# Two layers of a hybrid-attention transformer: remainders on GpSimd, queries split in whole tiles, and another order of the head groups' units

## The chip, the core and the metric

The kernel runs on one core of a Trainium2 chip. The metric is the device time of one execution in microseconds (us). The core has five engines, each with a queue that is worked off in order: TensorE (PE; its weight loads are shown as PEld), VectorE (DVE), ScalarE (ACT), GpSimd (POOL) and SyncE (SP), which here issues all transfers.

## The reference

Two layers of one trunk over 512 latent tokens (x) and 256 context tokens (ctx), width 1024, everything in float32. A layer is: modulation from SiLU(c) and SiLU(c_ctx); an RMS norm; one input projection of 3072 columns, split among four groups of heads; a mixer for each group; one output projection over the four results with a gated residual; an RMS norm and a squared-ReLU MLP of width 4096. Cut to what matters here:

```python
hx = rms_norm(x, p['norm1_g']) * (1 + sc1x) + sh1x
hc = rms_norm(ctx, p['norm1_g']) * (1 + sc1c) + sh1c
(lw_q, lw_k, lw_v, lf_q, lf_k, lf_v, lr_q, lr_k, lr_v, lr_g, ln_q, ln_k, ln_v) = split_in(hx @ p['w_in'])
...
out_w = window_attention(q, k, v, k_c, v_c, p['a_sink'])          # A
out_f = rms_norm(diff_attention(q, k, v, k_c, v_c, lam), ...)     # B
out_r = rms_norm(o_f + flip(o_b), p['c_gn_g']) * gate             # C
out_n = neighbourhood_attention(q, k, v, k_c, v_c, p['d_rpb'])    # D
mix_x = jnp.concatenate([...], axis=-1) @ p['w_out']
x = x + g1x * mix_x
x = x + g2x * squared_relu_mlp(h2, p['w_mlp1'], p['w_mlp2'])
```

A is windowed attention with a sink, B differential attention (two softmaxes of 32-wide halves, one subtracted from the other), C retention in both directions (no softmax, a decay table), D attention over a neighbourhood. In the second layer the context tokens only serve as keys and values.

## The kernel before

**Two parts for one number.** A matrix product in full precision is made of three in the format fp32r: every operand is split into a part hi (ScalarE copies the tile into fp32r) and a remainder lo = operand - hi (`split`, lines 275 and 276; the remainder by VectorE). `gemm` (lines 315 to 317) adds hi x hi, hi x lo and lo x hi. Activations h are held as pairs hh, hl; a weight tile (128 output columns by 1024 inputs) comes in two loads of 128x512, each into a buffer wr, and is split into wh and wl (`wload`). There are five buffers wr, which the loads of the modulation's weights share, and four each of wh and wl. In a layer's attention stage 24 weight tiles of the input projection and the first six eighths of eight tiles of the output projection pass through `wload`.

**Units.** Each group's work is cut into units: a0, b0, b1, c0, c1, d0, d1 (A has one, the others two of two heads each). A unit has an input part (`in_a` to `in_d`: its tiles of the input projection, norms, rotary tables, splits) and an attention part (`at_a` to `at_d`). `weave` runs the attention parts in the order `ORDER`, here a0 b0 b1 c0 c1 d0 d1, and lets the input parts of the following units, then the output projection (`out_ac`), run ahead of them by given leads. From the program written in this order, a scheduler sets the order of the instructions on each engine at build time; the engines then wait for each other by semaphores.

**Stacks.** A score is a product over 64 numbers (32 for B), so hi and lo of a query stand one above the other on the 128 partitions (`qs`), and the keys' hi (`ks`) and lo (`kl`) twice each. For A, C and D, `qstack` lets ScalarE write hi of a head's half tile and VectorE the remainder straight onto the other half (line 600); `kstack` does the same on one half (lines 608 and 610) and has the other half copied by a transfer from SBUF to SBUF (`KCOPY`, line 634, issued by SP), four for a tile. For B, `stack32` splits the whole tile into two tiles sp and puts four stacks together by 16 transfers of 32 partitions.

**Norms of heads.** `rstd` makes mean squares on TensorE (lines 241 and 243), `finish` the inverse roots on ScalarE and VectorE, which two products a piece (line 257) spread over the partitions again. Queries and keys of A, B and D pass through this on the way in, the outputs of B and C at the end of their unit (`headnorm`).

**GpSimd** does four small memsets and nothing else. In the MLPs, the weights go through the same `wload`.

## Time and profile before

| | |
|---|---|
| time, median of 3 runs | 1898.29 us (1894.59 to 1900.06) |
| the profiled execution | 1897.64 us, span of its instructions 1895.6 us |
| mean granted clock of TensorE | 0.990 |
| start and first norm | 0 to 70 us |
| attention stage, layer 0 | 70 to 540 us |
| MLP, layer 0 | 540 to 1090 us |
| attention stage, layer 1 | 1090 to 1560 us |
| MLP, layer 1 | 1560 to 1895.6 us |

The page of the profile gives each engine's busy time. [...] The timeline has each instruction with its start and length; in square brackets stands how long its engine was idle before it and what ended that. TensorE's instructions overlap, so the distance between two starts is what one takes of the engine's time, and the length shown is longer.

### The profile page before, as it was taken

The page shows a single profiled execution, that of the slowest core. Times are in us where ns is not written, and L with a number is a line of the kernel's source. Part 1 is how long each engine was busy: PE and PEld are TensorE (multiplying, and loading weights), DVE is VectorE, ACT ScalarE, POOL GpSimd, SP SyncE. Part 2 cuts the span into 40 slices and gives each one's busy share as a digit, 9 for nine tenths or more (in the row PEclk, how much of TensorE's full clock was granted, in tenths as well). Part 3 has the DMA queues.
Part 4 walks back from the last instruction along what each step waited for, and adds up shares of the span by engine and source line. Part 5 has one row for each costly group of instructions (what it writes and reads, how often), then busy time and mean ns, then how long its engine had stood idle before and what let it go on. Part 6 is the DMA issues. An engine that isn't in the chain of part 4 may idle for free.

```text
span 1895.6 us, 29665 instructions
## 1 busy us (share of the span) xinstructions
PE 1843.1 (97%) x10899; PEld 1519.8 (80%) x10899; DVE 1307.4 (69%) x3005; ACT 973.4 (51%) x1934; POOL 0.2 (0%) x4
## 2 busy tenths in 40 slices
PE   7998889999999999999999999999899999999999
PEld 3786667778878888888888777878677788989897
DVE  5788867788777847847847367898788764545453
ACT  4677656668654214223323356877577763334242
POOL 0000000000000000000000000000000000000000
PEclk8999989999999999999999999999899999999999
DMA  8324334432323523423422352332243223232322
GB/s 297 99 79 122 100 120 131 148 95 65 109 95 106 157 93 117 151 95 117 150 95 89 111 172 83 83 96 79 85 133 95 75 95 100 90 100 90 100 90 95
DMA packets 110417, 208.68 MB, mean 110 GB/s; under 512 B 14272, under 2 KB 20160, under 8 KB 110272
## 3 DMA queue, kind: packets, MB, share of 16 engines
q1 hardware_dynamic: 110272, 206.78, 34.7%
q8 instruction: 86, 1.41, 0.3%
q14 instruction: 59, 0.48, 0.1%
HBM read 182.09 MB, written 5.24 MB: 99 GB/s over the span
## 4 chain that ended last, share of the span: by engine, by line
PE 89%; ACT 5%; DVE 3%; DMA 2%; issue 1%; SPq 0%; ACTq 0%; DVEq 0%
PE mm L315 23%; PE mm L317 23%; PE mm L316 23%; PE ps L697 3%; PE po L703 2%; PE po L705 2%; PE ps L262 1%; PE ps L850 1%; PE pt L241 1%; ACT pth L275 1%; PE pt L257 1%; PE pt L869 1%; PE pt L798 1%; ACT P L856 1%; DMA zm<-in_dd_dram 1%
## 5 line engine op out<-in xcount | busy, mean ns | idle before, releaser
L275 ACT ACTIVATE wh<-wr 128x512 fp32r<-128x512 f32 (+1 forms) x414 | 252.9, 614 | 645.3 <-PE mm L316 605.0
L317 PE MATMUL mm<-hh,wl 128*128 128x512 f32 (+2 forms) x1680 | 548.8, 327 | 6.7 <-DVE wl L276 6.6
L315 PE MATMUL mm<-hh,wh 128*128 128x512 f32 (+2 forms) x1680 | 551.2, 328 | 3.0 <-ACT zq L651 1.7
L316 PE MATMUL mm<-hl,wh 128*128 128x512 f32 (+2 forms) x1680 | 549.8, 327 | 0.0
L276 DVE TENSOR_TENSOR wl<-wr,wh 128x512 fp32r<-128x512 f32 (+1 forms) x414 | 275.4, 667 | 162.4 <-ACT wh L275 156.4
L315 PEld LDWEIGHTS mm<-hh,wh 128*128 128x128 f32 x1680 | 318.3, 190 | 39.9 <-issue 7.6
L317 PEld LDWEIGHTS mm<-hh,wl 128*128 128x128 f32 x1680 | 318.9, 190 | 34.7 <-DVE wl L276 7.7
L316 PEld LDWEIGHTS mm<-hl,wh 128*128 128x128 f32 x1680 | 318.0, 189 | 28.1 <-issue 3.5
L316 PE MATMUL mm<-ml,wh 128*128 128x512 f32 (+1 forms) x768 | 273.2, 356 | 0.0
L315 PE MATMUL mm<-mh,wh 128*128 128x512 f32 (+1 forms) x768 | 272.7, 356 | 0.0
L317 PE MATMUL mm<-mh,wl 128*128 128x512 f32 (+1 forms) x768 | 272.4, 355 | 0.0
L316 PEld LDWEIGHTS mm<-ml,wh 128*128 128x128 f32 x768 | 145.2, 189 | 24.5 <-issue 4.5
L315 PEld LDWEIGHTS mm<-mh,wh 128*128 128x128 f32 x768 | 145.2, 189 | 21.9 <-issue 0.4
L317 PEld LDWEIGHTS mm<-mh,wl 128*128 128x128 f32 x768 | 145.1, 189 | 21.2 <-issue 1.2
L394 DVE SCALAR_TENSOR_TENSOR acc<-wm,silp,acc 128x512 f32<-128x512 f32 x196 | 138.9, 747 | 21.9 <-DMA wm<-in_wmod_dram 21.7
L1127 DVE SCALAR_TENSOR_TENSOR x<-mm,modc,x 128x512 f32<-128x512 f32 (+1 forms) x96 | 63.4, 660 | 116.6 <-PE mm L317 116.6
L703 PE MATMUL po<-pth,vv 128*128 128x256 f32 (+2 forms) x328 | 105.5, 328 | 8.9 <-ACT pth L275 8.1
L276 DVE TENSOR_TENSOR ptl<-pt,pth 128x512 fp32r<-128x512 f32 (+3 forms) x148 | 92.4, 630 | 27.9 <-ACT pth L275 26.4
L275 ACT ACTIVATE pth<-pt 128x512 fp32r<-128x512 f32 (+3 forms) x148 | 80.2, 547 | 32.2 <-PE pt L869 21.6
L1111 DVE TENSOR_TENSOR zq<-mm,nacc 128x256 f32<-128x256 f32 (+1 forms) x128 | 61.9, 484 | 44.5 <-PE mm L317 43.0
L703 PEld LDWEIGHTS po<-pth,vv 128*128 128x128 f32 x328 | 61.8, 189 | 32.3 <-ACT pth L275 24.0
L705 PE MATMUL po<-ptl,vv 128*64 128x256 f32 (+2 forms) x256 | 78.3, 318 | 2.9 <-DVE ptl L276 2.3
(251 smaller groups left out, 2701.3 us busy)
## 6 DMA issues: line engine op xcount, KB each, us to landing
wr<-in_w_dram SPq DMA_DIRECT2D x272, 256.0 KB, 2.6
wm<-in_wmod_dram SPq DMA_DIRECT2D x112, 256.0 KB, 2.8
wr<-in_win_dram SPq DMA_DIRECT2D x96, 256.0 KB, 3.0
wr<-in_wmodh_dram SPq DMA_DIRECT2D x48, 256.0 KB, 3.3
...
zm<-in_dd_dram SPq DMA_DIRECT2D x16, 256.0 KB, 3.5
```

The source lines that it names most:

```text
L241: T.matmul(pj, lhsT=gmean[w], rhs=sq[:, 256 * j:256 * j + 256], start=True, stop=add is None)
L275: S.activation(hi, src, AF.Copy)
L276: V.tensor_tensor(lo, src, hi.bitcast(F32), op=OP.subtract)
L315: T.matmul(p, lhsT=wh, rhs=ah[:, s:s + l], start=(k == 0), stop=False)
L316: T.matmul(p, lhsT=wh, rhs=al[:, s:s + l], start=False, stop=False)
L317: T.matmul(p, lhsT=wl, rhs=ah[:, s:s + l], start=False, stop=(k == len(act) - 1))
L394: V.scalar_tensor_tensor(acc[:, v], r, sil[:, k, v:v + 1], acc[:, v], op0=OP.mult, op1=OP.add)
L697: T.matmul(o, lhsT=x, rhs=y, start=(i == 0), stop=(i == 1))
L703: T.matmul(po[:, c0:c0 + l], lhsT=vv[:, hh, t], rhs=ph, start=start, stop=stop)
L705: T.matmul(po[0:64, c0:c0 + l], lhsT=vv[:, hh, t, 0:64], rhs=pl, start=False, stop=False)
L1111: V.tensor_tensor(r[:, s:s + l], p[:, :l], y2[:, s:s + l], op=OP.mult)
L1127: V.scalar_tensor_tensor(xx, p, modc[:, 40 + m, s // 512:s // 512 + 1], xx, op0=OP.mult, op1=OP.add)
```

## The change

- `split` takes the engine of the remainder as an argument. GpSimd (PL) makes the remainders of the weights in the attention stages (`wrest`; in the MLPs VectorE as before), of all queries and keys, and of the six outputs that `out_ac` splits; it also adds C's two tables (`ctables`). The remainders of the probabilities, of the values and of the norms stay on VectorE.
- Queries and keys of all groups are split as whole tiles into two tiles sp (`parts_of`) and put together by transfers (`stack`): a query tile of A, C or D takes four transfers of 64 partitions, a key tile eight. B's stay 16 of 32 partitions.
- There are six buffers zq instead of five (sp, squares, rotated tiles).
- `ORDER` is a0 c0 b0 c1 b1 d0 d1 in both layers. The numbers that `weave` takes for leads and costs are the same.

```diff
@@ -80,7 +80,7 @@
 PTB = 2
 PSB = 2
 POB = 1
-ZQ = 5
+ZQ = 6
 U3 = 20
 MID = 14
 WPRI = 40
@@ -100,7 +100,7 @@
 CD1 = 11
 TAILC = 10000.0
 MP = 7
-ORDER = ['a0 b0 b1 c0 c1 d0 d1', 'a0 b0 b1 c0 c1 d0 d1']
+ORDER = ['a0 c0 b0 c1 b1 d0 d1', 'a0 c0 b0 c1 b1 d0 d1']
 
 
 def weave(units, ins, ats, cost_in, cost_at, tail, lead, boost):
@@ -154,7 +154,7 @@
 @with_exitstack
 def body(ctx: ExitStack, tc, A):
     nc = tc.nc
-    V, S, G, T, SY = nc.vector, nc.scalar, nc.gpsimd, nc.tensor, nc.sync
+    V, S, PL, T, SY = nc.vector, nc.scalar, nc.gpsimd, nc.tensor, nc.sync
 
     cons = ctx.enter_context(tc.tile_pool(name="cons", bufs=1))
     main = ctx.enter_context(tc.tile_pool(name="main", bufs=1))
@@ -271,9 +271,11 @@
             V.scalar_tensor_tensor(sq[:, s:s + l], ap, EPS if eps else 0.0, sq[:, s:s + l], op0=OP.add, op1=OP.mult)
         V.scalar_tensor_tensor(sq[:, :n], sq[:, :n], -3.0, e3[:, :n], op0=OP.add, op1=OP.mult)
 
-    def split(src, hi, lo):
+    def split(src, hi, lo, eng=V):
         S.activation(hi, src, AF.Copy)
-        V.tensor_tensor(lo, src, hi.bitcast(F32), op=OP.subtract)
+        eng.tensor_tensor(lo, src, hi.bitcast(F32), op=OP.subtract)
+
+    wrest = [PL]
 
     def wload(src, k0=0, k1=8, dst=None):
 
@@ -288,7 +290,7 @@
                 hi = wp.tile([128, 512], F32R, name=nm("wh"), tag="wh", bufs=WB)
                 lo = wp.tile([128, 512], F32R, name=nm("wl"), tag="wl", bufs=WB)
             with tc.high_priority(offset=WPRI):
-                split(r, hi[:, :128 * n], lo[:, :128 * n])
+                split(r, hi[:, :128 * n], lo[:, :128 * n], wrest[0])
             res += [(hi[:, 128 * k:128 * k + 128], lo[:, 128 * k:128 * k + 128]) for k in range(n)]
         return res
 
@@ -467,6 +469,7 @@
         rb = rowb[:, L, :]
         modc = modcs[L]
 
+        wrest[0] = PL
 
         att = ExitStack()
         ap_ = att.enter_context(tc.tile_pool(name=f"att{L}", bufs=1))
@@ -591,44 +594,40 @@
 
         HALF = (slice(0, 64), slice(64, 128))
 
+        def parts_of(t, n):
+
+            hl = [main.tile([128, 768], F32R, name=nm("sp"), tag="zq", bufs=ZQ)[:, :n] for _ in range(2)]
+            split(t[:, :n], *hl, PL)
+            return hl
+
+        def stack(hl, n, r, order):
+
+            x, w = u3r("st"), r.stop - r.start
+            for i, o in enumerate(order):
+                KCOPY(x[w * i:w * i + w, :n], hl[o][r])
+            return x
+
         def qstack(t, n):
 
-            st = (u3r("qs"), u3r("qs"))
-            for h, x in enumerate(st):
-                a, b = HALF[h], HALF[1 - h]
-                S.activation(x[a, :n], t[a, :n], AF.Copy)
-                V.tensor_tensor(x[b, :n], t[a, :n], x[a, :n].bitcast(F32), op=OP.subtract)
-            return st
+            hl = parts_of(t, n)
+            return [stack(hl, n, r, (0, 1)) for r in HALF]
 
         def kstack(t, n):
 
-            st, lo = (u3r("ks"), u3r("ks")), (u3r("kl"), u3r("kl"))
-            for h, (x, y) in enumerate(zip(st, lo)):
-                a, b = HALF[h], HALF[1 - h]
-                S.activation(x[a, :n], t[a, :n], AF.Copy)
-                KCOPY(x[b, :n], x[a, :n])
-                V.tensor_tensor(y[a, :n], t[a, :n], x[a, :n].bitcast(F32), op=OP.subtract)
-                KCOPY(y[b, :n], y[a, :n])
-            return st, lo
+            hl = parts_of(t, n)
+            return [[stack(hl, n, r, (i, i)) for r in HALF] for i in range(2)]
 
         def quarter(i):
             return slice(32 * i, 32 * i + 32)
 
-        def stack32(t, n, order):
-
-            parts = [main.tile([128, 768], F32R, name=nm("sp"), tag="zq", bufs=ZQ)[:, :n] for _ in range(2)]
-            split(t[:, :n], *parts)
-            st = [u3r("st") for _ in range(4)]
-            for i, x in enumerate(st):
-                for r, w in enumerate(order):
-                    KCOPY(x[quarter(r), :n], parts[w][quarter(i)])
-            return st
-
         def qstack32(t, n):
-            return stack32(t, n, (0, 1, 0, 1))
+
+            hl = parts_of(t, n)
+            return [stack(hl, n, quarter(i), (0, 1, 0, 1)) for i in range(4)]
 
         def kstack32(t, n):
-            return stack32(t, n, (0, 0, 1, 1))
+            hl = parts_of(t, n)
+            return [stack(hl, n, quarter(i), (0, 0, 1, 1)) for i in range(4)]
 
         def KCOPY(dst, src):
             SY.dma_start(out=dst.bitcast(F32), in_=src.bitcast(F32))
@@ -912,7 +911,7 @@
                 SY.dma_start(out=tw[:, 0:512], in_=A['dd'][:, 1920 + 512 * t:2432 + 512 * t])
                 S.activation(tw[:, 0:512], tw[:, 0:512], AF.Exp, scale=nlb)
                 S.activation(tx[:, t], tx[:, t], AF.Exp, scale=lf)
-                V.tensor_tensor(tx[:, t], tx[:, t], tw[:, 0:512], op=OP.add)
+                PL.tensor_tensor(tx[:, t], tx[:, t], tw[:, 0:512], op=OP.add)
             return tb, tx
 
         def in_c(u):
@@ -1035,7 +1034,7 @@
             osp = []
             for c in range(6):
                 hi, lo = htile("oh"), htile("ol")
-                split(of[c][:, :nq], hi[:, :nq], lo[:, :nq])
+                split(of[c][:, :nq], hi[:, :nq], lo[:, :nq], PL)
                 osp.append((hi, lo))
             for m in range(8):
                 xr = u3("xr")
@@ -1055,6 +1054,7 @@
         cost_at = {x: c * 1e3 for x, c in zip('abcd', [[CA0, CB0, CC0, CD0], [CA1, CB1, CC1, CD1]][L])}
         weave(units, ins, ats, cost_in, cost_at, out_ac(), [[L0_0, L0_1, L0_2, L0_3, L0_4, L0_5, L0_6, L0_7], [L1_0, L1_1, L1_2, L1_3, L1_4, L1_5, L1_6, L1_7]][L], lambda: tc.high_priority(offset=BOOST))
         att.close()
+        wrest[0] = V
 
 
         mlp = ExitStack()
```

**On SP.** In these rows, wr is a weight load (L284 before, L286 after: projections; L373 and L375: modulation), and st<-sp, ks<-ks and kl<-kl are the transfers of the stacks. Before, where the queries of b1 (sp_2502, sp_2503) and the keys of c0 are put together:

```order
L634 DMA st_2509<-sp_2502 32x768
L634 DMA st_2509<-sp_2503 32x768
L634 DMA ks_2711<-ks_2711 64x768
L634 DMA kl_2713<-kl_2713 64x768
L634 DMA ks_2712<-ks_2712 64x768
L634 DMA kl_2714<-kl_2714 64x768
L284 DMA wr_2751<-in_win_dram 128x512
```

After, the end of the 16 transfers of b0's queries (sp_2399, sp_2400):

```order
L633 DMA st_2418<-sp_2399 32x768
L633 DMA st_2418<-sp_2400 32x768
L286 DMA wr_2445<-in_win_dram 128x512
L286 DMA wr_2451<-in_win_dram 128x512
L375 DMA wr_2559<-in_wmodh_dram 128x512
```

The next weights stand behind the transfers in both; after, the weights of the tile mm_2457 (c1's keys) are the first ones behind b0's queries, and both halves of that tile stand there.

**On TensorE, the end of b0 in layer 0.** The products of the output's norm (L241, L243; spread by L257). Before:

```order
L703 MATMUL po_2810<-pth_2816,vv_1291 128x256
L241 MATMUL ps_2839<-zm_2836,gmean_75 32x256
L243 MATMUL ps_2839<-ident,lsq_2833 32x128 x2
L241 MATMUL ps_2839<-zm_2836,gmean_75 32x256
L243 MATMUL ps_2839<-ident,lsq_2833 32x128 x2
L241 MATMUL ps_2839<-zm_2836,gmean_75 32x256
L243 MATMUL ps_2839<-ident,lsq_2833 32x128 x2
L257 MATMUL ps_2838<-rr_2840,spread 128x256
```

After (L684 transposes values, L344 is the modulation, L317 to L319 is `gemm`):

```order
L243 MATMUL ps_3473<-ident,lsq_3467 32x128 x2
L684 MATMUL pt_3722<-ident,zq_3718 128x128 x4
L344 MATMUL mm_3745<-wr_3737,silp 32x256
L684 MATMUL pt_3732<-ident,zq_3718 128x128 x2
L344 MATMUL mm_3745<-wr_3737,silp 32x256
L344 MATMUL mm_3745<-wr_3739,silp 32x256 x2
L344 MATMUL mm_3745<-wr_3741,silp 32x256
L257 MATMUL ps_3472<-rr_3474,spread 128x256
```

Before, nothing stands between the mean squares and the spread; after, six transposes and five small products do, and tile mm_3771 follows.

**On TensorE, the end of c0 in layer 0, after.** Scores are L696, probabilities times values L701 to L704:

```order
L702 MATMUL po_2328<-pth_2603,vv_1164 128x512
L704 MATMUL po_2328<-ptl_2604,vv_1164 64x512
L701 MATMUL po_2328<-ptl_2627,vv_1164 64x512
L702 MATMUL po_2328<-pth_2626,vv_1164 128x512
L702 MATMUL po_2641<-pth_2647,vv_1164 128x256
L704 MATMUL po_2641<-ptl_2648,vv_1164 64x256
L701 MATMUL po_2641<-ptl_2671,vv_1164 64x256
L702 MATMUL po_2641<-pth_2670,vv_1164 128x256
L317 MATMUL mm_2457<-hh_217,wh_2447 128x512
L318 MATMUL mm_2457<-hl_218,wh_2447 128x512
```

The last products of c0 come right before tile mm_2457, whose weights are those behind the 16 transfers above.

**The weights' remainders in layer 1.** On VectorE before, at the end of b0's attention (L600 a query remainder, L933 and L934 c0's gate):

```order
L600 TENSOR_TENSOR qs_14141<-zq_14138,qs_14141 64x512
L879 TENSOR_TENSOR of_13829<-po_14011,ev_14087 64x256
L853 TENSOR_SCALAR sm_14111<-sm_14111 128x2
L853 TENSOR_SCALAR sm_14090<-sm_14090 128x2
L933 SCALAR_TENSOR_TENSOR zq_14184<-zq_14184,zq_14187 128x512
L903 TENSOR_SCALAR zm_14198<-gp_14194,lg_11949 128x128
L934 SCALAR_TENSOR_TENSOR gt_14183<-gt_14183,gsc_11929,zq_14184 128x512
L904 TENSOR_SCALAR gp_14194<-gp_14194,nlg_11983 128x128
L276 TENSOR_TENSOR wl_14427<-wr_14424,wh_14426 128x512
```

On GpSimd after, in layer 1:

```order
L276 TENSOR_TENSOR wl_13910<-wr_13907,wh_13909 128x512
L276 TENSOR_TENSOR sp_13683<-zq_13679,sp_13682 128x768
L276 TENSOR_TENSOR wl_14024<-wr_14021,wh_14023 128x512
L276 TENSOR_TENSOR sp_14012<-zq_14009,sp_14011 128x512
L276 TENSOR_TENSOR wl_14030<-wr_14027,wh_14029 128x512
```

There the weights' remainders (wl) share a queue with those of queries and keys (sp) alone: 128 wl, 30 sp, 12 of the outputs and 16 sums of tables in both layers.

## Rows read from the trace of the kernel before

**Rows 1.** Page, busy time of each engine, share of span, instructions.
```profile
PE 1843.1 (97%) x10899; PEld 1519.8 (80%) x10899; DVE 1307.4 (69%) x3005; ACT 973.4 (51%) x1934; POOL 0.2 (0%) x4
```

**Rows 2.** Stretches: us, busy PE, PEld, DVE, ACT, POOL, clock, DMA share, GB/s.
```profile
70.00:234.00 164.00, 154.52 (x1014) 124.27 (x1012) 134.98 (x416) 119.90 (x271) 0.00 (x0) 1.00 0.36 101
234.00:256.00 22.00, 14.04 (x53) 9.13 (x54) 11.79 (x32) 9.00 (x20) 0.00 (x0) 0.69 0.36 107
256.00:540.00 284.00, 279.51 (x1718) 224.27 (x1716) 226.44 (x546) 190.94 (x406) 0.00 (x0) 1.00 0.36 112
1090.00:1330.00 240.00, 236.09 (x1390) 189.41 (x1388) 192.57 (x507) 165.79 (x340) 0.00 (x0) 1.00 0.35 102
1330.00:1358.00 28.00, 20.27 (x88) 15.28 (x87) 23.72 (x60) 15.86 (x33) 0.00 (x0) 0.82 0.32 95
1358.00:1560.00 202.00, 199.38 (x1128) 156.06 (x1127) 154.53 (x348) 142.89 (x293) 0.00 (x0) 1.00 0.32 99
```

**Rows 3.** Timeline, layer 0, 234 to 256 us: start, length, idle time before.
```profile
239.58 0.58 SPq L284 DMA_DIRECT2D wr<-in_win_dram  x1
...
240.78 1.06 PE L241 MATMUL ps<-zm,gmean 128*32 128x256 f32 x2 [1.79 <-ACT zm L817]
...
247.15 0.61 ACT L275 ACTIVATE wh<-wr 128x512 fp32r<-128x512 f32 x1
...
247.29 1.28 PE L257 MATMUL ps<-rr,spread 96*128 96x256 f32 x6 [2.87 <-ACT rr L275]
```

**Rows 4.** Timeline, layer 1, 1331 to 1352 us, VectorE and TensorE.
```profile
1331.62 0.69 DVE L600 TENSOR_TENSOR qs<-zq,qs 64x512 fp32r<-64x512 f32 x1
...
1334.47 0.67 DVE L276 TENSOR_TENSOR wl<-wr,wh 128x512 fp32r<-128x512 f32 x1
...
1335.19 0.79 PE L317 MATMUL mm<-hh,wl 128*128 128x512 f32 x1 [3.17 <-DVE wl L276]
...
1349.34 0.95 DVE L610 TENSOR_TENSOR kl<-zq,ks 64x768 fp32r<-64x768 f32 x1
...
1350.41 0.67 DVE L276 TENSOR_TENSOR wl<-wr,wh 128x512 fp32r<-128x512 f32 x1
...
1351.14 0.80 PE L317 MATMUL mm<-hh,wl 128*128 128x512 f32 x1 [3.39 <-DVE wl L276]
```

**Rows 5.** Groups by form on VectorE, 70 to 540 us: busy us, mean ns.
```profile
L276 DVE TENSOR_TENSOR wl<-wr,wh 128x512 fp32r<-128x512 f32 x48 | 32.7, 684 | 6.3 <-ACT wh L275 6.2
...
L276 DVE TENSOR_TENSOR ptl<-P,pth 128x512 fp32r<-128x512 f32 x24 | 16.4, 685 | 2.9 <-ACT pth L275 2.8
...
L600 DVE TENSOR_TENSOR qs<-zq,qs 64x768 fp32r<-64x768 f32 x12 | 11.4, 953 | 1.6 <-ACT qs L599 1.2
...
L610 DVE TENSOR_TENSOR kl<-zq,ks 64x768 fp32r<-64x768 f32 x10 | 9.5, 950 | 0.6 <-ACT ks L608 0.4
...
L667 DVE TENSOR_TENSOR zq<-zq,pt 128x512 f32<-128x512 f32 x11 | 7.6, 687 | 6.1 <-PE pt L257 6.1
```

**Rows 6.** Groups by form on ScalarE, 70 to 540 us.
```profile
L275 ACT ACTIVATE sp<-zq 128x768 fp32r<-128x768 f32 x4 | 3.3, 837 | 2.8 <-DVE zq L667 2.8
```

**Rows 7.** Timeline of SP's transfers between SBUF tiles, layer 0.
```profile
73.61 1.16 SPq L634 DMA_DIRECT2D kl<-kl  x2
...
103.89 11.28 SPq L634 DMA_DIRECT2D st<-sp  x16
...
176.41 10.05 SPq L634 DMA_DIRECT2D st<-sp  x16
```

**Rows 8.** DMA issues: count, KB each, median us to landing.
```profile
wr<-in_win_dram SPq DMA_DIRECT2D x96, 256.0 KB, 3.0
...
ks<-ks SPq DMA_DIRECT2D x20, 192.0 KB, 2.9
```

**Rows 9.** Timeline of TensorE in layer 0's MLP: start and length.
```profile
702.30 0.39 PE L317 MATMUL mm<-hh,wl 128*128 128x512 f32 x1
702.53 0.39 PE L315 MATMUL mm<-hh,wh 128*128 128x512 f32 x1
```

## Prediction

> **What bounds the kernel now.** TensorE is busy for 97% of the span and VectorE for 69% [rows 1], so the most that a change can win is what TensorE loses. The table by stretches says where that is: I leave out the start (0 to 70 us) and the two MLPs, since the change leaves them as they are but for four weight remainders, and look at the two attention stages, which are 940 us of the span. TensorE is busy there for 903.8 us of 940, idle for 36.2 us [rows 2]. The idle time is not spread evenly: 8.0 us of it lie in 22 us of layer 0 (234 to 256 us) and 7.7 us in 28 us of layer 1 (1330 to 1358 us), and only these two stretches have a mean granted clock under 1.00, of 0.69 and 0.82 [rows 2]. [...] In time at full speed that is up to 0.31 x 22 = 6.8 us and 0.18 x 28 = 5.0 us; only the share in which TensorE was busy counts (0.64 and 0.72), so 4.4 and 3.6 us. The two places cost about 12.4 and 11.3 us, the rest of both stages has 20.5 us of idle time.
>
> The timeline says why. In layer 1 TensorE waits twice, 3.17 and 3.39 us, for a weight remainder wl. VectorE made each in 0.67 us, but took it up only behind a query remainder (L600, 0.69 us) and other work the first time, and directly behind a key remainder (L610, 0.95 us) the second time [rows 4]: an engine that works in order had the weights in the wrong place of its queue. In layer 0 unit b0 ends: its norm's chain makes TensorE wait 1.79 us and 2.87 us, and there is nothing to fill it, since the next weights were issued by SP only at 239.58 us, behind 20 copies, and ScalarE reached them at 247.15 us [rows 3].
>
> **The change part by part.** *Remainders leave VectorE.* In the attention stages these go: 128 weight remainders (112 of 512 columns, 16 of 256), 112 x 0.684 + 16 x 0.34 = 82 us; 24 query remainders, 12 x 0.953 and 12 shorter ones at about two thirds, 19 us; 20 key remainders x 0.95 = 19 us; B's eight splits, 16 table sums and twelve output splits, about 28 us by the same times per column [rows 5]. VectorE's 744 us of 940 (79%) [rows 2] become about 596 (63%). Directly on the path lie the two waits of layer 1: 6.6 us of idle time and 3.6 us of clock. GpSimd's queue holds 186 remainders and nothing else, so the weights no longer stand behind scores and gates. Something else on VectorE is late next there (the next ptl), so I take 9 of the 10.2 us (bounds 5 and 10).
>
> What one remainder takes on GpSimd no row shows. Below I bound it with VectorE's own time, 0.68 us for 512 columns and 0.95 us for 768, and with twice that; I take 1.7 us for 768 columns, near the upper end, because for the sum only a late remainder matters. All 186 are 131 us at the lower bound and 261 us at the upper, 14 to 28% of 940 us: GpSimd does not become the bound. [...]
>
> The relief acts on the other 20.5 us of idle time as well, where TensorE waits for short steps of VectorE and ScalarE. I take 12 us of it (bounds 0 and 18), since VectorE's free time rises from 21 to 37%.
>
> *B alternates with C.* b0 is now followed by c1 and not by b1. At b0's end the products of tile mm_3771 stand next, with weights that SP issued before any copy, and six transposes and five products lie inside the norm's chain; so 12.4 us go and some 3 us of the 4.7 us of waits [rows 3] stay: -9.4 us.
>
> The same kind of hole opens elsewhere. In the new SP order all 16 copies of b0's queries stand ahead of wr_2445, the next weights (before, one tile of weights was fetched ahead of such a block). From the last spread product on, the chain is: VectorE's two products, 0.69 + 0.41 us [rows 5]; ScalarE's copy 0.84 us [rows 6]; GpSimd's remainder 1.7 us, of which one copy's issue hides 0.6; 16 copies 10.6 us (10.05 to 11.28) [rows 7]; landing 3.0 us [rows 8]; wh 0.6 us [rows 3]. Sum 17.2 us. TensorE has between these the tail of c0: 12 products of 512 columns at 0.23 us [rows 9], eight of 256 at half of it, and six narrow ones, together 4.3 us. So it loses 12.9 us, and with the same clock loss as in the hole before (4.4 us) 17 us. Bounds: 11.6 (remainder at 0.95 us, 10.05 us of copies, full clock) and 18.2.
>
> Elsewhere in c0 and c1 of layer 0 some seven chunks stand without input products between them. One chunk costs VectorE two operations of 0.685 us [rows 5], TensorE 4 x 0.23 = 0.92 us; 7 x 0.45 = 3 us (bounds 0 and 6).
>
> *Queries in whole tiles.* Each of 12 query tiles of A, C and D now goes over four copies, where ScalarE and VectorE wrote the stacks directly, and each of 10 key tiles over eight instead of four: 88 more, at 0.58 us of SP each [rows 7] 51 us, plus a landing of 2.9 us [rows 8]. In most places another unit's attention covers this. It is open where the unit follows at once: a0 in both layers, and d1, four tiles; about 1.3 us each, +5 us (bounds 0 and 12). A wait of SP here holds up the weight loads that stand behind it. ScalarE wins a little, since one copy of 0.84 us [rows 6] takes the place of two as long: nothing on the path.
>
> The sum: -9 - 12 - 9.4 + 17 + 3 + 5 = -5.4 us. The profiled execution took 1897.64 us (span 1895.6), 0.65 us under the median of 1898.29 us, so 1897.64 - 5.4 = **1892 us**.
>
> **The rivals.** *More of the idle time goes.* If the relief is at its bound (18 us), the queries' copies are all covered and the hole is at its lower bound, it gives 1892 - 6 - 5 - 5 = about 1876 to 1880 us. For it: VectorE is the engine that both other waits in layer 1 end at [rows 4]. Against: the order has more stretches without input products in layer 0 than before.
>
> *The relief is given back at a shared port.* VectorE keeps some 190 operations with two inputs in SBUF (ptl from P, the rotary tables, P from P). If such an operation and a GpSimd remainder exclude each other, then with 28% of the time taken each waits 0.28 x 0.7 = 0.2 us, 38 us of VectorE, and the remainders on GpSimd are late as well. Then the 12 us of relief are lost: 1904 us. [...]
>
> *Slower: SP's copies hold up the weights.* In layer 1, 40 copies (b0's keys and queries, c1's keys) stand in one block ahead of wr_14027: 40 x 0.65 = 26 us of SP, and chain and landing make it 33 us from b0's keys to the products that need these weights. The order leaves about 30 us of TensorE's work between c1's keys, the last of the three, and these products, and b0's keys are ready before. If SP starts the block late, because it waits for GpSimd, a second hole opens there: 8 us and 4.4 us of clock, and the queries' copies are then at their upper end, +7 us: 1892 + 19 = 1911 us. It decides from the point where the last copies start over 10 us after c1's keys are split. For it: SP's block before b1 ended in the hole at 234 us [rows 3]. Against: a tile and a half of weights is issued ahead of that block.
>
> **How the numbers follow.** Under 0.3% (5.7 us) can't be told from no change here: the bounds are 1892.6 and 1904.0 us. Forecast (1886 to 1898 us) 0.36, of which 0.20 under the bound; more gain (1880) 0.22; port (1904) 0.16, half on either side; copies (1911) 0.26. So faster 0.20 + 0.22 = 0.42, same 0.16 + 0.08 = 0.24, slower 0.08 + 0.26 = 0.34. Since both signs hold much, the forecast's own range is 1886 to 1898 us; 8 in 10 need both gains and the copies' case nearly to its middle: 1876 to 1910 us.
>
> **What would show it.** Right: no wait of TensorE for wl of 3 us in layer 1; VectorE near 600 us in the attention stages; in layer 0 one wait of TensorE before mm_2457 of 8 to 13 us, with SP's 16 copies before it and a clock under 1.00 after it; b0's end without a hole of 5 us. Wrong: no hole there (then the time is near 1880); a GpSimd remainder of over 1.4 us for 512 columns, or ptl and P operations of VectorE that last longer than 0.69 and 1.01 us (port); a second hole of layer 1 in b0 or c1 behind the 40 copies (slower).

## The result and the profile after

The changed kernel takes 1950.02 us (median of 4 runs, 1944.58 to 1951.72) against 1897.48 us: a ratio of 1.027, with a 95% interval of 1.025 to 1.030. It is 2.7% or 52.5 us slower. The forecast was 1892 us and the range ended at 1910 us. (One execution of one experiment further below, gpsimd_paced, took 10012.64 us and stands apart; the other nine took 1889.43 to 1899.33 us.)

The profiled execution took 1948.49 us, its span is 1946.6 us. The page, busy time of each engine (answers [rows 1]):

```profile
PE 1862.8 (96%) x10899; PEld 1520.1 (78%) x10899; DVE 1238.7 (64%) x2797; ACT 954.9 (49%) x1912; POOL 258.8 (13%) x190
```

Where the 51 us of the span came in can be read from the same instruction in both kernels. The last update of x in layer 0's output projection (L1084), on VectorE's timeline, before and then after:

```profile
559.16 0.48 DVE L1084 SCALAR_TENSOR_TENSOR x<-mm,modc,x 128x256 f32<-128x256 f32 x1
```

```profile
597.57 0.48 DVE L1084 SCALAR_TENSOR_TENSOR x<-mm,modc,x 128x256 f32<-128x256 f32 x1
```

So 38.4 us came in before the end of layer 0's attention stage. The table by stretches, cut so that both kernels do the same work in a row (2113 products of TensorE in the second), shows 12 us more for layer 1's stage and, between its rows, 574 instead of 573 us for layer 0's MLP. Its columns are us, busy PE, PEld, DVE, ACT, POOL, clock, DMA share, GB/s. Before:

```profile
70.00:560.00 490.00, 468.08 (x2884) 369.82 (x2882) 388.30 (x1024) 333.75 (x728) 0.00 (x0) 0.99 0.35 106
1133.00:1533.00 400.00, 385.74 (x2113) 300.41 (x2112) 324.58 (x828) 285.30 (x593) 0.00 (x0) 0.99 0.32 94
```

After:

```profile
70.00:598.00 528.00, 487.87 (x2897) 375.55 (x2896) 351.95 (x929) 324.75 (x720) 121.95 (x85) 0.97 0.40 115
1172.00:1584.00 412.00, 389.05 (x2113) 298.30 (x2112) 290.93 (x727) 277.76 (x583) 121.61 (x90) 0.99 0.38 109
```

TensorE's idle time rose from 21.9 to 40.1 us and from 14.3 to 23.0 us; the rest is busy time, part of it at the lower clock (0.97 instead of 0.99 in layer 0). VectorE's busy time fell by only 70 us (712.9 to 642.9 us), though operations of 148 us by their lengths had left it. The lengths of VectorE's operations overlap (their sum is 1468 us for 1307 us of busy time before, 1380 us for 1239 us after), so they don't come off the busy time one for one. Compared form by form with the run of five buffers zq and all remainders on VectorE (further below), the operations that stayed on VectorE are 61 us longer in all: some 60 of the 148 us were given back. The groups by form of the whole span after show where: remainders with two inputs in SBUF and with one (pt is in PSUM), the softmax's P from P, a small scaling, a reciprocal of the same shape, and GpSimd's own work.

```profile
L276 DVE TENSOR_TENSOR ptl<-pt,pth 128x512 fp32r<-128x512 f32 x116 | 79.1, 687 | 34.4 <-ACT pth L275 33.1
...
L276 DVE TENSOR_TENSOR ptl<-P,pth 128x512 fp32r<-128x512 f32 x48 | 40.4, 846 | 4.5 <-ACT pth L275 3.1 <-PE po L702 1.1
...
L859 DVE SCALAR_TENSOR_TENSOR P<-P,sm,P 128x768 f32<-128x768 f32 x32 | 36.2, 1132 | 0.3
...
L749 DVE TENSOR_SCALAR sm<-sm 128x2 f32<-128x2 f32 x40 | 12.8, 319 | 0.6
...
L756 DVE RECIPROCAL sm<-sm 128x2 f32<-128x2 f32 x40 | 6.4, 160 | 8.0 <-ACT P L751 7.8
```

The same before (ptl from P is in [rows 5]):

```profile
L276 DVE TENSOR_TENSOR ptl<-pt,pth 128x512 fp32r<-128x512 f32 x116 | 79.3, 688 | 25.8 <-ACT pth L275 24.9
...
L860 DVE SCALAR_TENSOR_TENSOR P<-P,sm,P 128x768 f32<-128x768 f32 x32 | 32.3, 1011 | 0.2
...
L750 DVE TENSOR_SCALAR sm<-sm 128x2 f32<-128x2 f32 x40 | 6.5, 162 | 0.2
L757 DVE RECIPROCAL sm<-sm 128x2 f32<-128x2 f32 x40 | 6.4, 161 | 2.1 <-ACT P L752 1.8
```

GpSimd after:

```profile
L276 POOL TENSOR_TENSOR wl<-wr,wh 128x512 fp32r<-128x512 f32 x110 | 149.9, 1368 | 1052.0 <-ACT wh L275 994.0 <-PE pt L797 13.0 <-PE mm L318 8.9
L276 POOL TENSOR_TENSOR sp<-zq,sp 128x768 fp32r<-128x768 f32 x22 | 42.4, 1928 | 93.8 <-ACT sp L275 58.4 <-PE mm L319 14.3 <-issue 12.3
```

The remainder from PSUM is as long as before (0.69 us). The one from P, the same operation with both inputs in SBUF, went from 0.68 to 0.85 us, P from P from 1.01 to 1.13 us. The small scaling has one input and doubles as well (0.16 to 0.32 us), the reciprocal of the same shape doesn't (0.16 us in both). On GpSimd a weight remainder takes 1.37 us and one of 768 columns 1.93 us, twice VectorE's time (0.68 and 0.95 us [rows 5]). Of the prediction's signs of its port rival, the longer operations ptl and P are there; a GpSimd remainder of over 1.4 us for 512 columns is just missed.

The predicted hole is there too. SP, GpSimd, ScalarE and TensorE after, at the end of c0 in layer 0:

```profile
221.98 11.92 SPq L633 DMA_DIRECT2D st<-sp  x16
234.00 1.01 SPq L286 DMA_DIRECT2D wr<-in_win_dram  x2
```

```profile
222.08 1.83 POOL L276 TENSOR_TENSOR sp<-zq,sp 128x768 fp32r<-128x768 f32 x1 [8.82 <-issue]
```

```profile
236.97 0.63 ACT L275 ACTIVATE wh<-wr 128x512 fp32r<-128x512 f32 x1 [6.07 <-DMA wr<-in_win_dram]
```

```profile
237.65 0.80 PE L317 MATMUL mm<-hh,wh 128*128 128x512 f32 x1 [7.17 <-ACT wh L275]
```

The chain is the predicted one, with 16 transfers ahead of the next weights. It costs 7.2 us, not 12.9 us. From the end of the last spread products, at 220.1 us, it took 17.5 us:

```profile
219.50 0.64 PE L257 MATMUL pt<-rr,spread 96*128 96x256 f32 x4
```

The prediction had 17.2 us. But TensorE's own work, scores and products of the modulation among it, went on to 230.5 us beside the chain, with some 2 us of short waits.

The table by stretches around this hole and at the end of b0 in layer 0, where the products of the output's norm stand, after:

```profile
228.00:248.00 20.00, 11.36 (x52) 8.81 (x52) 2.82 (x5) 6.17 (x12) 3.80 (x3) 0.74 0.69 208
332.00:345.00 13.00, 9.81 (x78) 6.62 (x73) 6.39 (x15) 7.36 (x17) 1.81 (x1) 1.00 0.25 63
```

The hole at c0's end takes another 0.26 x 11.4 = 3 us by the clock. At b0's end 3.2 us are idle, at full clock.

### The profile page after: what moved, and what is told of

It reads as the page before. It is cut to its first block, busy times and chain, and to the rows that moved or that the text cites. A ratio compares the mean times of both kernels' runs of the same rounds, so it can differ in the third digit from the quotient of the medians.

```text
span 1946.6 us, 29951 instructions
## 1 busy us (share of the span) xinstructions
PE 1862.8 (96%) x10899; PEld 1520.1 (78%) x10899; DVE 1238.7 (64%) x2797; ACT 954.9 (49%) x1912; POOL 258.8 (13%) x190
## 5 line engine op out<-in xcount | busy, mean ns | idle before, releaser
L317 PE MATMUL mm<-hh,wh 128*128 128x512 f32 (+2 forms) x1680 | 551.7, 329 | 8.4 <-ACT wh L275 8.2
L319 PE MATMUL mm<-hh,wl 128*128 128x512 f32 (+2 forms) x1680 | 549.5, 327 | 3.0 <-POOL wl L276 2.6
L317 PEld LDWEIGHTS mm<-hh,wh 128*128 128x128 f32 x1680 | 318.2, 190 | 45.3 <-ACT wh L275 9.0
L319 PEld LDWEIGHTS mm<-hh,wl 128*128 128x128 f32 x1680 | 318.3, 189 | 35.9 <-POOL wl L276 6.0
L276 POOL TENSOR_TENSOR wl<-wr,wh 128x512 fp32r<-128x512 f32 x126 | 162.5, 1297 | 1074.8 <-ACT wh L275 1012.5
L276 DVE TENSOR_TENSOR wl<-wr,wh 128x512 fp32r<-128x512 f32 (+1 forms) x288 | 193.9, 673 | 144.1 <-ACT wh L275 139.9
L317 PE MATMUL mm<-mh,wh 128*128 128x512 f32 (+1 forms) x768 | 272.5, 355 | 0.0
L319 PE MATMUL mm<-mh,wl 128*128 128x512 f32 (+1 forms) x768 | 272.1, 354 | 0.0
L318 PEld LDWEIGHTS mm<-ml,wh 128*128 128x128 f32 x768 | 145.1, 189 | 24.5 <-issue 4.5
L317 PEld LDWEIGHTS mm<-mh,wh 128*128 128x128 f32 x768 | 145.1, 189 | 22.0 <-issue 0.4
L319 PEld LDWEIGHTS mm<-mh,wl 128*128 128x128 f32 x768 | 145.1, 189 | 21.2 <-issue 1.2
L696 PE MATMUL ps<-st,st 128*128 128x256 f32 (+2 forms) x400 | 104.0, 338 | 3.5 <-DMA st<-sp 1.4
L704 PE MATMUL po<-ptl,vv 128*64 128x256 f32 (+2 forms) x256 | 79.9, 324 | 9.6 <-DVE ptl L276 9.2
```

The lines of the kernel that those rows point to most:

```text
L276: eng.tensor_tensor(lo, src, hi.bitcast(F32), op=OP.subtract)
L317: T.matmul(p, lhsT=wh, rhs=ah[:, s:s + l], start=(k == 0), stop=False)
L318: T.matmul(p, lhsT=wh, rhs=al[:, s:s + l], start=False, stop=False)
L319: T.matmul(p, lhsT=wl, rhs=ah[:, s:s + l], start=False, stop=(k == len(act) - 1))
L696: T.matmul(o, lhsT=x, rhs=y, start=(i == 0), stop=(i == 1))
L704: T.matmul(po[0:64, c0:c0 + l], lhsT=vv[:, hh, t, 0:64], rhs=pl, start=False, stop=False)
```

## The experiments

Times are medians; the ratio is to the kernel before on the same chip, with its 95% interval. "Step" below is the difference between two medians. The runs come from several chips; beside them the kernel before had medians of 1897.88 to 1899.53 us.

### The three parts, each alone

```diff
-ORDER = ['a0 b0 b1 c0 c1 d0 d1', 'a0 b0 b1 c0 c1 d0 d1']
+ORDER = ['a0 c0 b0 c1 b1 d0 d1', 'a0 c0 b0 c1 b1 d0 d1']
```

> The kernel before with the order a0 c0 b0 c1 b1 d0 d1 and nothing else; all remainders stay on VectorE, the stacks are built as before. Order theory (the alternation leaves the units of the later half of layer 0 without input products between their short steps): most of the 52 us, 1930 to 1950 us. GpSimd theory (slow remainders there, and VectorE's operations stretched beside them): within 10 us of before, 1888 to 1908 us. Copies theory (88 more transfers between SBUF tiles hold up weights and scores): also within 10 us, since the hole before mm_2457 is then shorter by the remainder only.

Measured: 1923.45 us, 1.0141 (1.0126 to 1.0157), +24 us. About half of the loss.

```diff
-                split(r, hi[:, :128 * n], lo[:, :128 * n])
+                split(r, hi[:, :128 * n], lo[:, :128 * n], wrest[0])
...
-            split(t[:, :n], *parts)
+            split(t[:, :n], *parts, PL)
```

(So too the sums of the tables and the outputs; old order, and queries and keys of A, C and D as before.)

> The kernel before with the remainders of the weights, of B's whole tiles, of the six outputs and the sums of C's tables on GpSimd in the attention stages; old order, and A, C and D's queries and keys as before (ScalarE and VectorE write the stacks). GpSimd theory: 1.37 us instead of 0.68 us for a weight remainder and VectorE's operations with two SBUF inputs stretched by 10 to 25% cost 15 to 30 us: 1912 to 1928 us. Order and copies theories: a gain as in the forecast's terms of minus 9 and minus 12, or nothing: 1876 to 1900 us.

Measured: 1906.46 us, 1.0047 (1.0032 to 1.0062), +7 us: a loss where the forecast had its largest gains, but a smaller one than the GpSimd theory said.

```diff
-        eng.tensor_tensor(lo, src, hi.bitcast(F32), op=OP.subtract)
+        V.tensor_tensor(lo, src, hi.bitcast(F32), op=OP.subtract)
```

(This line, the same in the tables, and the old order, in the changed kernel.)

> Queries and keys of A, C and D split in whole tiles and put together by transfers, six buffers zq; all remainders on VectorE, old order. Copies theory: 15 to 30 us slower, 1912 to 1928 us, with the wait of the scores or of the weights behind the transfers. Order and GpSimd theories: within 8 us of before (the prediction's own term was plus 5): 1890 to 1906 us.

Measured: 1894.43 us, 0.9974 (0.9964 to 0.9984), -5 us. With 88 more transfers the kernel is no slower in the old order, so the copies theory falls there; what the transfers cost and what whole tiles save elsewhere is not told apart.

> The changed kernel with the old order a0 b0 b1 c0 c1 d0 d1: remainders on GpSimd and whole tiles together. Order theory: 1876 to 1900 us, the 52 us are gone. GpSimd and copies theories together: 1930 to 1950 us; one of them alone leaves 1912 to 1930 us. If the parts only hurt together (a late remainder on GpSimd holds up the transfers, these hold up the weights behind them on SP), it is slower than the sum of the other two of this group.

Measured: 1922.72 us, 1.0132 (1.0116 to 1.0147), +23 us (the changed kernel with the order's line as before). The order (+24) and the other two parts together (+23) add up to the 52 us but for 5 us. From whole tiles alone to this kernel the remainders on GpSimd cost 28 us.

Where does the order lose? The table by stretches of the run with the order alone, layer 0 (columns as above):

```profile
210.00:240.00 30.00, 22.48 (x115) 15.88 (x116) 11.89 (x21) 12.17 (x22) 0.00 (x0) 0.89 0.65 185
240.00:290.00 50.00, 49.01 (x312) 37.73 (x311) 38.02 (x119) 31.38 (x68) 0.00 (x0) 1.00 0.37 114
290.00:330.00 40.00, 34.15 (x203) 25.29 (x201) 31.70 (x81) 23.55 (x53) 0.00 (x0) 0.87 0.26 77
330.00:400.00 70.00, 65.89 (x342) 45.85 (x341) 51.59 (x121) 37.55 (x75) 0.00 (x0) 1.00 0.51 148
400.00:440.00 40.00, 36.66 (x220) 28.70 (x219) 37.08 (x117) 32.02 (x75) 0.00 (x0) 1.00 0.08 26
440.00:480.00 40.00, 39.98 (x270) 33.65 (x268) 32.62 (x91) 32.94 (x70) 0.00 (x0) 1.00 0.20 59
480.00:520.00 40.00, 37.17 (x235) 31.55 (x233) 31.36 (x97) 34.99 (x84) 0.00 (x0) 0.91 0.21 66
```

There are two holes now. At c0's end (210 to 240 us) 7.5 us are idle, and the clock takes 0.11 x 22.5 = 2.5 us. At b0's end (290 to 330 us) 5.9 us are idle and 0.13 x 34.2 = 4.4 us go with the clock. From 330 to 520 us another 10 us are idle, and 3.3 us go with the clock; before, the whole stretch from 256 to 540 us had 4.5 us of idle time [rows 2]. The hole at b0's end is no longer in the norm but one step earlier, in the last softmax (TensorE's timeline of the same run):

```profile
307.32 0.69 PE L869 MATMUL pt<-ident,P 128*128 128x128 f32 x2 [1.46 <-DVE P L860]
309.84 1.54 PE L869 MATMUL pt<-ident,P 128*128 128x128 f32 x6 [1.83 <-DVE P L860]
```

VectorE works there almost without a pause, on maxima, scalings and P from P, and between two of the latter on a shuffle (0.72 us) and a rotary product (0.68 us) of an input part; TensorE has no product ready to do beside it.

### Which remainders cost, and the sixth buffer

In the next two, with whole tiles, old order and six buffers zq, only the weights' remainders go to GpSimd, or only those of queries and keys.

```diff
-            split(t[:, :n], *hl, PL)
+            split(t[:, :n], *hl)
```

(So too the tables and the outputs.)

> Whole tiles, old order, and of the remainders only the weights' on GpSimd. The step from whole tiles alone (1894.4 us) to all remainders on GpSimd (1922.7 us) is 28 us, and this run and the next part it. Port theory (the cost is VectorE's operations, stretched while GpSimd works): it goes by GpSimd's busy time, of which the weights have some 163 of 260 us, so +18 us, 1912 us. Lateness theory (the remainders of queries and keys come late, with 1.93 us instead of 0.95 us on a path that ends in transfers): +4 to +8 us, 1898 to 1902 us, or a gain, since the weights leave VectorE's queue.

Measured: 1906.31 us, 1.0039 (1.0026 to 1.0052), a step of +12 us from whole tiles alone.

```diff
-        wrest[0] = PL
+        wrest[0] = V
```

> Whole tiles, old order, and of the remainders only those of queries and keys (tiles sp) on GpSimd. Port theory: 78 of 260 us of GpSimd, +8 us, 1902 us. Lateness theory: most of the 28 us, +18 to +24 us, 1912 to 1918 us, with the waits of TensorE for transfers st or for weights behind them.

Measured: 1907.91 us, 1.0048 (1.0033 to 1.0062), a step of +13 us. Each is about half; neither theory as it was put holds for both.

```diff
-ZQ = 6
+ZQ = 5
```

> Whole tiles alone with five buffers zq, as before the change. It is the base of the next run, which needs the room, and shows what the sixth buffer is worth: if the 5 us that whole tiles win come from it, 1899 us or more; if they come from ScalarE's shorter work, 1892 to 1897 us.

Measured: 1880.06 us, 0.9903 (0.9885 to 0.9921). Whole tiles with the old number of buffers are 19 us faster than the kernel before and 70 us faster than the changed one: this version beats both. One more buffer costs 14 us, and the build orders TensorE's instructions otherwise with it. The table over b0's end in layer 0 shows one place, six buffers and then five:

```profile
240.00:270.00 30.00, 25.03 (x113) 15.05 (x111) 18.32 (x59) 13.47 (x28) 0.00 (x0) 0.72 0.38 112
```

```profile
235.00:265.00 30.00, 27.59 (x161) 20.58 (x162) 23.27 (x72) 17.23 (x39) 0.00 (x0) 0.89 0.40 112
```

With five buffers TensorE does 161 products in 30 us there instead of 113, at a clock of 0.89 instead of 0.72: the hole of [rows 3] is mostly filled. In idle time and clock that is some 7 of the 14 us.

### What GpSimd's work does by itself

```diff
+        V.tensor_tensor(lo, src, hi.bitcast(F32), op=OP.subtract)
+        if eng is PL:
+            PL.tensor_tensor(scr[:, :n], hi.bitcast(F32), hi.bitcast(F32), op=OP.subtract)
```

> As the run with five buffers zq, all remainders on VectorE; beside each remainder that the change moves, GpSimd does a subtraction of the same shape from the same hi tile into a tile that nobody reads. So GpSimd is as busy as in the changed kernel and nobody waits for it. Port theory: VectorE's operations get longer (P from P over 1.1 us instead of 1.01, ptl from P over 0.75 instead of 0.68) and the time rises by 15 us or more over the run with five buffers. Lateness theory: at most 5 us over it.

Measured: 1952.63 us, 1.0282 (1.026 to 1.0303), a step of +73 us over five buffers. But it isn't clean: the tile wh can't be reused before GpSimd has read it, and the waits show ScalarE standing for that:

```profile
ACT wh L275 <- POOL scr L279: 38.4, 26, 4.6
```

The next kernel reads one column of the finished wl and then works on a private tile.

> Whole tiles, five buffers zq, old order, all remainders on VectorE; behind each of the 128 weight remainders GpSimd reads one column of it and then subtracts a private tile of 128x512 (128x256) from itself. So GpSimd works as long as in the run before, no result of it is read, and it holds no buffer of weights while it works (in the run with idle work ScalarE waited 38 us for such buffers, so that run overstates the port). Port theory: VectorE's operations beside it get longer and the time rises by 8 us or more, 1888 us or more. Lateness theory: 1878 to 1884 us.

Measured: 1929.45 us, 1.0161 (1.0141 to 1.0181), a step of +49 us. The pieces had no wait of their own and ran in a bunch; the table by stretches shows POOL at 61 of 70 and 85 of 90 us, and hardly any after:

```profile
0.00:70.00 70.00, 38.93 (x222) 21.65 (x222) 62.43 (x145) 21.79 (x41) 61.13 (x63) 0.78 0.56 202
70.00:160.00 90.00, 72.38 (x381) 54.50 (x381) 76.01 (x119) 36.34 (x79) 84.99 (x81) 0.91 0.35 98
160.00:300.00 140.00, 135.92 (x881) 106.15 (x879) 114.04 (x370) 102.17 (x237) 4.72 (x15) 0.99 0.43 121
```

In that bunch VectorE's timeline has longer operations (the norm's first step, two in 2.17 us, where one takes 0.75 us in the run with five buffers, and a weight remainder in 1.53 us, 0.69 us there):

```profile
67.03 2.17 DVE L447 SCALAR_TENSOR_TENSOR zq<-x,gs,nacc 128x512 f32<-128x512 f32 x2
...
83.06 1.53 DVE L276 TENSOR_TENSOR wl<-wr,wh 128x512 fp32r<-128x512 f32 x1
```

TensorE, ScalarE and SP have the order of the run with five buffers, but for two products of TensorE that changed places, and TensorE has done 602 products by 160 us where that run had done 959. So work on GpSimd that nobody reads delays TensorE by itself, through VectorE. The size had to be taken again, with the pieces paced by the weights (the column goes into the private tile, so each piece waits for its own) and in two doses:

```diff
+                    PL.tensor_tensor(scr[:, 0:1], lo[:, 0:1].bitcast(F32), lo[:, 0:1].bitcast(F32), op=OP.subtract)
+                    s = scr[:, :128 * n]
+                    PL.tensor_tensor(s, s, s, op=OP.subtract)
```

> Whole tiles, five buffers zq, old order, all remainders on VectorE; behind each of the 128 weight remainders GpSimd copies nothing but one column of it and then subtracts a private tile of that width from itself, and now each such piece waits for its own weights (in the last run the pieces ran in a bunch before 115 us). The order of the instructions on TensorE, ScalarE and SP is that of the run with five buffers. Port theory: VectorE's operations with two SBUF inputs get longer, and 1880 us become 1890 us or more. Theory of another order (what costs is that the build orders TensorE's and VectorE's work otherwise when a remainder moves): 1878 to 1884 us.

Measured: 1892.85 us, 0.9972 (0.9958 to 0.9987), a step of +13 us.

```diff
                     PL.tensor_tensor(s, s, s, op=OP.subtract)
+                    PL.tensor_tensor(s, s, s, op=OP.subtract)
```

> The run gpsimd_paced with two such subtractions behind each weight remainder, some 300 us of GpSimd (the changed kernel has 259 us). Port theory: the rise over 1880 us is about twice that of the single dose, 1900 us or more. Theory of another order: at most 8 us, 1888 us.

Measured: 1915.15 us, 1.0086 (1.0069 to 1.0103), a step of +35 us. The pages of the run with five buffers, of one dose and of two:

```profile
PE 1840.2 (98%) x10899; PEld 1518.0 (81%) x10899; DVE 1288.6 (69%) x2983; ACT 951.7 (51%) x1912; POOL 0.2 (0%) x4
```

```profile
PE 1848.1 (98%) x10899; PEld 1520.3 (80%) x10899; DVE 1319.4 (70%) x2984; ACT 952.4 (50%) x1912; POOL 185.0 (10%) x260
```

```profile
PE 1852.0 (97%) x10899; PEld 1517.9 (79%) x10899; DVE 1358.2 (71%) x2984; ACT 953.5 (50%) x1912; POOL 334.4 (17%) x388
```

TensorE, ScalarE and SP have the same order of instructions in all three, and VectorE does the same operations but for one that clears the private tile, some of the first ones in another order. VectorE's busy time gets 31 and 70 us longer. P from P and both remainders with two inputs in SBUF got longer, and the remainder from PSUM did not (groups by form, five buffers and then two doses):

```profile
L276 DVE TENSOR_TENSOR wl<-wr,wh 128x512 fp32r<-128x512 f32 x382 | 262.2, 688 | 164.4 <-ACT wh L275 159.3 <-PE pt L684 0.5 <-PE po L701 0.2
...
L859 DVE SCALAR_TENSOR_TENSOR P<-P,sm,P 128x768 f32<-128x768 f32 x32 | 32.3, 1013 | 0.1
```

```profile
L276 DVE TENSOR_TENSOR wl<-wr,wh 128x512 fp32r<-128x512 f32 x382 | 275.9, 724 | 163.2 <-ACT wh L275 154.6 <-issue 1.6 <-POOL scr L297 0.8
...
L276 DVE TENSOR_TENSOR ptl<-pt,pth 128x512 fp32r<-128x512 f32 x116 | 79.1, 686 | 17.6 <-ACT pth L275 16.5
...
L866 DVE SCALAR_TENSOR_TENSOR P<-P,sm,P 128x768 f32<-128x768 f32 x32 | 36.8, 1154 | 0.1
L276 DVE TENSOR_TENSOR ptl<-P,pth 128x512 fp32r<-128x512 f32 x48 | 34.8, 727 | 1.8 <-ACT pth L275 1.6
```

These forms, with their narrower ones, have some 27 of the 72 us that the lengths grew by in all; the rotary products, the norms' small steps and the scalings have much of the rest. So the longer operations that the port theory forecast are there without lateness and without another order of TensorE; a port itself no run shows. For the 259 us of GpSimd in the changed kernel the line between the doses gives 13 + (259 - 185) / (334 - 185) x 22 = 24 us, an estimate. It is a loose one, since the bunch of the run before cost 49 us with 184 us of GpSimd. With VectorE's growth by forms in the place of GpSimd's time (31 and 72 us for the doses, 61 us for the changed kernel) the line gives 29 us.

Two real placements on the same base (the two edits above, of the weights alone and of queries and keys alone, with ZQ = 5):

> Whole tiles, five buffers zq, old order, and only the weights' remainders on GpSimd (128 in the attention stages). With six buffers this step cost 12 us (1906 against 1894 us). Port theory and lateness theory both: about 1880 + 12 = 1892 us; the next run tells them apart. The prediction's term for the weights alone was a gain of 9 us: 1871 us.

Measured: 1911.42 us, 1.0074 (1.0056 to 1.0093), a step of +31 us.

> Whole tiles, five buffers zq, old order, and of the remainders only those of queries and keys on GpSimd (30 of them, 52 us). With six buffers this step cost 13 us (1908 against 1894 us). Port theory by GpSimd's time: 52 of 166 us of the weights' run, which cost 31 us: +10 us, 1890 us. Theory of another order: anything from 1880 to 1910 us, with the loss in one or two places and not spread.

Measured: 1907.48 us, 1.0045 (1.0031 to 1.0059), a step of +27 us with only 52 us of GpSimd. VectorE's longer operations can't be all of that. The build also sets another order of instructions here, and b0's end in layer 0 is open again. The table over it, weights and then queries and keys:

```profile
245.00:275.00 30.00, 24.45 (x114) 15.45 (x113) 18.68 (x58) 13.33 (x29) 2.10 (x2) 0.72 0.42 116
```

```profile
240.00:270.00 30.00, 23.47 (x103) 13.56 (x102) 18.42 (x60) 12.38 (x27) 0.00 (x0) 0.72 0.43 122
```

Against five buffers (2.4 us idle, 0.11 x 27.6 = 3.0 us of clock) that is 3 to 4 us more idle time and, with 6.8 and 6.6 us of clock, some 4 us more at the lower clock: 7 to 8 us of the 31 and 27 us. VectorE's operations that stayed grew by 50 and 12 us by forms, for which the line of the doses gives some 23 and 5 us, an estimate, less what the relief is worth. Nearly all is lost in layer 0: at the last update of x there (L1084) the two runs stand 29 and 22 us behind the one with five buffers. How these steps are shared among VectorE's longer operations, late remainders and the other order isn't settled.

### The relief of VectorE, and the order

```diff
-                split(r, hi[:, :128 * n], lo[:, :128 * n])
+                S.activation(hi[:, :128 * n], r, AF.Copy)
+                lo = hi
```

> The kernel before, in which the remainders of the weights are left out in the attention stages (the product with lo takes wh again; the result is then another), so that 128 operations leave VectorE, some 82 us, and GpSimd does nothing. Theory of relief (the prediction's terms of -9 us for the waits for weights and -12 us for VectorE's free time, of which the weights are some 6 us): 1880 to 1886 us. If VectorE's free time is worth nothing because other steps of the chains end last: 1892 to 1900 us. A build that orders TensorE's work otherwise can move either by some 13 us, the price of one hole at the end of b0; then the place in the trace shows it.

Measured: 1866.13 us, 0.9827 (0.9809 to 0.9846), -32 us, twice what the theory of relief said. TensorE's wait for wl, 6.6 us before, is gone in the attention stages. In the table for layer 1's stage TensorE is idle for 3.6 us of 397 us (14.3 us of 400 us in the kernel before), at full clock:

```profile
1103.00:1500.00 397.00, 393.43 (x2223) 310.73 (x2224) 305.26 (x788) 293.31 (x611) 0.00 (x0) 1.00 0.35 103
```

So the relief exists, and with it the value of 82 us of VectorE; moved to GpSimd, the same remainders cost 12 or 31 us instead. (The remainder is also never late in this run, and the order of the build differs, so the 32 us are not VectorE's time alone.)

The order was looked at on the base of five buffers, all remainders on VectorE (the line `ORDER` as changed, ZQ = 5).

> Whole tiles, five buffers zq, all remainders on VectorE, and the new order. Order theory (the new order costs the same whatever lies beside it; alone it cost 24 us): 1880 + 24 = 1904 us. If the order's cost was that of B's units alone while ScalarE wrote the stacks itself, or if whole tiles take from it the hole before mm_2457: 1880 to 1892 us. If the sixteen transfers of each of B's tiles and the 88 new ones meet: over 1910 us.

Measured: 1915.64 us, 1.0084 (1.0058 to 1.011), a step of +36 us: more than on the old kernel. This fits a base that has almost no hole at b0's end to lose, which no run shows by itself.

The changed kernel with ZQ = 5 in place of 6:

> The changed kernel with five buffers zq instead of six. In the old order with all remainders on VectorE the sixth buffer cost 14 us (1894 against 1880 us). If that holds here: 1950 - 14 = 1936 us. If it was an accident of one place (the hole at the end of b0 in layer 0, which the new order does not have), 1947 to 1953 us; if a GpSimd remainder of 1.93 us holds the buffers longer, so that six are wanted: over 1953 us.

Measured: 1949.16 us, 1.0275 (1.0256 to 1.0293), like the changed kernel (1950.02 us). The sixth buffer's 14 us belong to the old order with all remainders on VectorE: with the weights on GpSimd six buffers are 5 us faster than five (1906 and 1911 us), with queries and keys on GpSimd they make no difference (1908 and 1907 us).

```diff
-L0_1 = 0.35
-L0_2 = 0.45
-L0_3 = 0.35
-L0_4 = 0.3
-L0_5 = 0.25
+L0_1 = 0.55
+L0_2 = 0.65
+L0_3 = 0.55
+L0_4 = 0.5
+L0_5 = 0.45
```

> Whole tiles, five buffers zq, all remainders on VectorE, the new order, and layer 0's leads of the positions 1 to 5 raised by 0.2 (0.55, 0.65, 0.55, 0.5, 0.45 instead of 0.35, 0.45, 0.35, 0.3, 0.25). Theory of leads (the numbers belong to the old order; the end of b0 and b1 has no input products left): 1915 us fall by 10 us or more, below 1905 us. Theory of the order itself (copies of b0's queries ahead of the next weights, B's last chunk on its own): 1910 to 1925 us, since more input ahead only moves the place.

Measured: 1930.87 us, 1.0168 (1.015 to 1.0185), 15 us slower than with the old leads. Leads that are too small are not the cause. Smaller ones were not tried.

```diff
-WR = 5
+WR = 6
```

> Whole tiles, five buffers zq, all remainders on VectorE, the new order, and six buffers wr for loads of weights instead of five. Theory of the SP block (in layer 0 the next weights stand behind b0's sixteen transfers, TensorE waits 4.9 us for wh at 227 us): one more load gets ahead of the block, this wait goes, and 1915 us become 1903 to 1910 us. Theory of the chain (TensorE has too little other work at c0's and b0's end, whatever the weights do): 1911 to 1920 us.

Measured: 1914.78 us, 1.0073 (1.0051 to 1.0095), no change. The wait for wh at 227 us went, and a longer one came three us later, for the modulation's weights, which stood behind the same block of transfers. TensorE with five buffers wr, then with six, and SP with six:

```profile
226.98 0.79 PE L317 MATMUL mm<-hh,wh 128*128 128x512 f32 x1 [4.92 <-ACT wh L275]
```

```profile
230.20 1.31 PE L344 MATMUL mm<-wr,silp 128*32 128x256 f32 x6 [6.17 <-DMA wr<-in_wmodh_dram]
```

```profile
206.94 19.40 SPq L633 DMA_DIRECT2D st<-sp  x24
226.44 2.60 SPq L375 DMA_DIRECT2D wr<-in_wmodh_dram  x4
```

One more buffer passes one load ahead of the block and no more; the block of 24 transfers, 19 us of SP, is what the hole follows.

## Why the prediction was wrong, point by point

The step that failed first of all is that work moved to GpSimd leaves VectorE's time. The remainders on GpSimd were to win 21 us (-9 and -12); from whole tiles alone to the same with all remainders on GpSimd they cost 28 us. That is 49 of the 58 us between forecast and result. The order cost 24 us where its terms had 10.6 us (13 us more), whole tiles won 5 us where the term had cost 5 us (10 us less), and the parts together cost 5 us more than one by one.

**-9, weights leave VectorE's queue.** The mechanism was right. After, TensorE waits for a wl five times, 2.6 us in all and 1.0 us at most, where two waits of 3.17 and 3.39 us had stood [rows 4]:

```profile
PE mm L319 <- POOL wl L276: 2.6, 5, 1.0
```

**-12, relief of VectorE.** The relief exists (32 us for the weights' share when nothing is given back), but the step that failed is the one behind it: that work moved to GpSimd leaves VectorE's time. Of the 148 us that went, some 60 us came back as longer operations of VectorE. The rival of the port had a chance of 0.16, and its price was put at the lost relief, 12 us; the paced doses give 24 to 29 us for the changed kernel, an estimate, on top of the relief. One of its signs came: ptl from P rose over 0.69 us and P from P over 1.01 us. The other, a remainder on GpSimd of over 1.4 us for 512 columns, was just missed at 1.37 us. The upper bound of a GpSimd remainder, twice VectorE's time, was reached (1.37 us for 512 columns, 1.93 us for 768). The rival's own figure for VectorE's wait, 0.28 x 0.7 us for some 190 operations, is 38 us; it was 61 us, and the forms that the rival named (ptl from P, the rotary tables, P from P) have some 20 of them. Overlooked were the small ones: a scaling of 128x2 went from 0.16 to 0.32 us (40 of them, in the softmax of A and D), B's from 0.16 to 0.25 us.

That the two engines share a port or exclude each other was the rival's supposition, and no run shows a port. What the trace of the changed kernel shows is the lengths (128x512): the 16 ptl from P that overlap an instruction of GpSimd took 1.18 us on average, the 32 others 0.68 us; of ptl from PSUM the 27 that overlap one took 0.69 us, like the 89 others.

**-9.4, the hole at b0's end goes.** Right in the changed kernel: 3.2 us of idle time at full clock are left (332 to 345 us) of the 12.4 us, as forecast. It doesn't hold for the order by itself. In the run of the order alone the hole moved from the norm to the last softmax of b0, at 10 us: I had looked at what stands between the steps of the norm and not at the chunk ahead of it. In the changed kernel products of the input projection still lie beside that softmax.

**+17, a new hole before mm_2457.** Right in place and chain, too large: 7.2 us of wait and 3 us of clock instead of 12.9 and 4.4 us in the changed kernel, about 10 us with the clock in the run of the order alone too. The term that was mis-sized is TensorE's own work beside the chain, which lasted 10 us and not 4.3 us; the chain's 17.2 us were right (17.5 us). The 1.7 us in it for a remainder of 768 columns on GpSimd were an estimate that no row showed; the changed kernel has 1.83 us at this place and 1.93 us on average. In the run of the order alone the two holes together are the 20 us (3 + 17) that the prediction left for them, by two errors that cancel, which is luck; in the changed kernel they are some 13 us.

**+3, chunks without input products.** This term was far too small. From 330 to 520 us the order alone has 10 us of idle time and 3 us of clock where the kernel before had 4.5 us of idle time in a longer stretch, and layer 1 adds about 5 us. With b0's end it makes the order's +24 us where the terms had +10.6 us.

**+5, copies of the queries.** Wrong in sign on the old order: -5 us with six buffers, -19 us with five. In sum the transfers cost nothing there; what they can do is stand ahead of weights, and that depends on the order.

**The rival of a second hole in layer 1 behind 40 transfers** didn't come: layer 1 lost only 12 us, in many waits of under 3 us. The time is beyond it since two causes that I had each priced as a single case came together: VectorE's longer operations beside GpSimd (24 to 29 us by the doses, an estimate, and the relief that didn't come) and the order (24 us).

**Left open:** how the cost of the remainders on GpSimd beyond VectorE's longer operations divides between their lateness (1.37 us for 0.67 us) and the other order that the build then sets, and why nearly all of it lies in layer 0.
